# The matrices of a grouped state-space scan built with real and imaginary parts side by side in three vector operations, a sum of two scans handed to an adding DMA, and padded copies moved to ScalarE

## The chip, the cores and the metric

One core of a Trainium2 chip runs the whole program in one launch. Its engines run side by side, each through its own list in order: TensorE (PE, matrix products), VectorE (DVE), ScalarE (ACT), GpSimd (POOL) and SyncE (SP). Waits between them are semaphores. SP, ACT and POOL also issue DMAs, each from its own queue, and a DMA that waits holds everything behind it in that queue. The metric is device microseconds of one execution, lower is better. Everything is float32 in and out.

## The reference, cut to what matters

One block of a diffusion model: a mixer with two parallel head groups, then an MLP. The mixer's products `u @ w_in` give the inputs of an RG-LRU group (8 heads of 128 channels), its gates, and the inputs of an S5 group (64 channel groups of 16). Of the RG-LRU:

```python
def coeffs(xc):                       # xc: conv of 4 taps over time
    r = sigmoid(block_diag_linear(xc, wa, ba))
    i = sigmoid(block_diag_linear(xc, wi, bi))
    log_a = -8 * softplus(-lam) * r
    return exp(log_a), sqrt(-expm1(2 * log_a)) * (i * xc)
# linear scan forward and backward, each: 256 context steps, then 1024 latent steps
rg_lat = (hl_f + hl_b) * gelu(gate_lat)          # the sum of the two directions
```

Of the S5 group, per channel group g, with 64 complex states in two directions:

```python
lam_bar = exp(lam * dt)
b_bar = ((lam_bar - 1) / lam)[..., None] * (b_re + 1j * b_im)
bu = einsum("blgh,gph->blgp", u, b_bar)          # into the states
h = scan of h[t] = lam_bar * h[t - 1] + bu[t]
y = einsum("blgp,ghp->blgh", h, c_re + 1j * c_im).real
```

Then GELU, a gated linear unit, one output product `w_out`, a layer norm, and the MLP with a second norm.

## The kernel before, in words

Channels lie on the 128 partitions, time along the free dimension. float32 products are made of three passes: every operand is split into a high part and a rest (`wh`, `wl`, `x0h`, `x0l`; ScalarE casts the high part, L98, VectorE subtracts it, L47), and TensorE multiplies high by high, high by rest and rest by high. L47 is the line of the helper `tt`, through which nearly all two-operand VectorE work goes, so it is told apart by tile names. `x0h`, `x0l` are the latent tokens (512 columns a product), `x1h`, `x1l` the context (256).

S5 is not scanned step by step over time but in chunks of 8 tokens. For each of eight blocks m of 8 channel groups the kernel builds three things from the powers `pw` of `lam_bar`, the input matrix `bb` (b_bar) and the output matrix `cc`:
- X (`make_x`, `make_xt`, L487 to L514): `bb` times eight powers, complex, for four groups at a time: six operations of 128 x 512 on VectorE (`X0`, `X1`, temporary `Xt`), then eight transposes on TensorE (`ps_tr`, L510), ScalarE copies (`xt`, L511) and a store to memory. It is later the matrix that carries a chunk into the states.
- Y (`s5_taps`, L516 on): `cc` times eight powers, again four groups at a time, six operations (`Y`, temporary `yt`), with `cn`, the negated imaginary part; stored by SP as `yd` and later read as `yf`, the matrix from states to outputs.
- the taps inside a chunk: Y times a zero-padded copy `bz` of `bb` (8 small VectorE copies for each block, L561; products `ps_kt`, L566; ScalarE copy `kt`, L569).

These are interleaved with the RG-LRU heads in one stage (74 to 420 us). The program text calls its steps in the order of the string `X0 R0 T0 G2 S0 R1 X1 S1 T1 R2 X2 ... T3 X4 R4 ...` (L576), where R is a head (`rg_head`, L409), G the projection of a head's input (`proj_rgx`), S the projection of a block's S5 input (`proj_s5`); T is `s5_taps`, X is `make_xt`. From this text, a scheduler sets at build time each engine's list. Tiles of one tag with `bufs=1` share one buffer, so the next writer waits for the last reader.

A head R runs a chain. ScalarE and VectorE make the conv (`xc`: one activation, three multiply-adds, L56), ScalarE rounds it (`xch`, L421), VectorE forms the rest (`xcl`), TensorE makes 36 gate products (`ps_g`, L435), ScalarE takes sigmoids (`rr`, `ii`, L437), then, with two loads of its function table, Exp (`aa`, L442), Tanh (L443) and Sqrt (`rr`, L446); VectorE multiplies (`rr`, `ii`) and runs three scans (L455 to L458), and adds the two directions (`ii`, L47). The sum goes to memory as `hs` on SP's queue (L462; head 7's on POOL's). The next head's conv stands on VectorE among the scans of this one. The eight heads begin 41 to 46 us apart.

After the last head, `s5_in` (L592) loads X and the inputs, makes the products `ps_si` (L601) and copies them into `H` (the states of blocks 0 to 3 by ScalarE and VectorE, those of 4 to 7 by ScalarE alone). `scan` (L608) is some 128 dependent steps of three small VectorE operations for each half, preceded by a tree over the context (`sC`). Beside it TensorE makes the gates (`proj_gate`, `ge`; it reads `hs`) and the output products, then the S5 outputs `ps_so` (L751 to L753), which need `H`, and all that follows (norm, MLP), which the change does not touch.

Of the kernel before, what the change touches and what calls it, by code (L numbers as in the profile page):

```python
# [41 lines left out]
def build(nc, tc, a, out):  # L42
# [1421 lines left out]
```

## Time and profile before

| | |
|---|---|
| time, median of 3 runs | 1595.54 us (1594.12 to 1600.06) |
| the profiled execution | 1594.69 us, of it a span of 1592.9 us |
| TensorE busy | 1476.7 us (93%) |
| VectorE busy | 1256.8 us (79%) |
| ScalarE busy | 843.0 us (53%) |
| GpSimd busy | 71.0 us (4%) |
| mean granted TensorE clock | 0.974 of full |

Busy time is the time in which an engine ran at least one instruction; matmuls overlap in TensorE's pipeline, so a mean duration of 395 ns does not mean one each 395 ns. An average over the program hides its stages: the stage of the heads has TensorE and VectorE equally busy (326.90 us of 346 each, by chance the same figure), the scans that follow bind VectorE, and from about 680 us on TensorE hardly ever rests. A row of a wait names the engine and line that waited, and what came last.

### The profile page before, as it was taken

The numbers are of one execution on the slowest core, as the hardware profiler recorded it, in microseconds if no ns is written. First come the engines' busy times: TensorE is split into PE (matmuls) and PEld (weight loads), VectorE is DVE, ScalarE is ACT, GpSimd is POOL, SyncE is SP. The second block draws the span as 40 slices with busy tenths as digits, with TensorE's granted clock in tenths as the row PEclk, the third lists the DMA queues.
The fourth block names the chain that finished last, engine by engine and source line by source line (L and its number), as shares of the span: only waits on it lengthen the run. The fifth ranks groups of instructions, "written<-read, shape, count | busy, mean of one in ns | idle before, by whom it ended". The sixth has DMA issues, their size and how long they took to land. (4 is left out here: it accounts for less than half of the span.)

```text
span 1592.9 us, 20440 instructions
## 1 busy us (share of the span) xinstructions
PE 1476.7 (93%) x7148; PEld 1202.4 (75%) x7148; DVE 1256.8 (79%) x2555; ACT 843.0 (53%) x1178; POOL 71.0 (4%) x141
## 2 busy tenths in 40 slices
PE   7899998999978999699999799989899899999997
PEld 2687777778756878598878677867788788888886
DVE  7899999998866989635978789778787566667877
ACT  4675656666795331954233576444555554344425
POOL 0000000000000000000000011111111000000000
PEclk9999999999999999799999999999999999999999
DMA  7623323323664752983768576777764786776703
GB/s 255 233 94 119 115 99 120 105 106 119 231 215 137 209 183 91 264 201 119 228 207 265 173 242 232 279 248 268 245 219 167 268 287 215 263 251 210 240 7 106
DMA packets 131382, 304.16 MB, mean 191 GB/s; under 512 B 16208, under 2 KB 47440, under 8 KB 129872
## 3 DMA queue, kind: packets, MB, share of 16 engines
q1 hardware_dynamic: 104048, 237.45, 46.9%
q0 software_dynamic: 13184, 47.72, 8.4%
q10 hardware_dynamic: 14048, 17.70, 3.1%
q8 instruction: 56, 0.92, 0.2%
q14 instruction: 46, 0.38, 0.1%
HBM read 219.52 MB, written 83.30 MB: 190 GB/s over the span
## 5 line engine op out<-in xcount | busy, mean ns | idle before, releaser
L98 ACT CAST wh<-wr 128x1024 fp32r<-128x1024 f32 x113 | 118.4, 1051 | 230.0 <-PE ps_m L1276 73.8
L47 DVE TENSOR_TENSOR wl<-wr,wh 128x1024 fp32r<-128x1024 f32 (+1 forms) x161 | 170.5, 1060 | 83.7 <-ACT wh L98 77.2
L1066 PE MATMUL ps_m<-xt,wh 128*128 128x512 f32 x512 | 160.7, 395 | 0.0
L1276 PE MATMUL ps_m<-bh,wh 128*128 128x512 f32 x392 | 153.7, 392 | 3.8 <-ACT bh L1238 3.7
L1276 PE MATMUL ps_m<-bl,wh 128*128 128x512 f32 x392 | 153.4, 391 | 0.5 <-DVE bl L47 0.5
L1276 PE MATMUL ps_m<-bh,wl 128*128 128x512 f32 x392 | 153.3, 391 | 0.0
L380 PE MATMUL ps_mm<-x0h,wh 128*128 128x512 f32 x352 | 140.3, 399 | 1.0 <-ACT wh L98 1.0
L380 PE MATMUL ps_mm<-x0h,wl 128*128 128x512 f32 x352 | 140.0, 399 | 0.9 <-DVE wl L47 0.9
L380 PE MATMUL ps_mm<-x0l,wh 128*128 128x512 f32 x352 | 140.0, 398 | 0.0
L1066 PEld LDWEIGHTS ps_m<-xt,wh 128*128 128x128 f32 x512 | 97.5, 191 | 21.2 <-issue 0.3
L1066 PE MATMUL ps_m<-xt,wl 128*128 128x512 f32 x256 | 101.9, 398 | 10.5 <-DVE wl L47 10.5
L1276 PEld LDWEIGHTS ps_m<-bh,wh 128*128 128x128 f32 x392 | 73.8, 188 | 20.6 <-ACT bh L1238 4.1
L1276 PEld LDWEIGHTS ps_m<-bl,wh 128*128 128x128 f32 x392 | 74.0, 189 | 16.6 <-DVE bl L47 1.0
L1276 PEld LDWEIGHTS ps_m<-bh,wl 128*128 128x128 f32 x392 | 74.0, 189 | 15.5
L675 PE MATMUL ps_wo<-ms,wh 128*128 128x512 f32 x256 | 81.7, 400 | 2.7 <-ACT ms L799 2.7
L1066 PE MATMUL ps_m<-x,wh 128*128 128x512 f32 x256 | 81.8, 400 | 1.0 <-ACT wh L1149 1.0
L380 PEld LDWEIGHTS ps_mm<-x0h,wl 128*128 128x128 f32 x352 | 67.2, 191 | 14.3 <-DVE wl L47 1.4
L380 PEld LDWEIGHTS ps_mm<-x0h,wh 128*128 128x128 f32 x352 | 67.1, 191 | 13.5 <-ACT wh L98 1.4
L380 PEld LDWEIGHTS ps_mm<-x0l,wh 128*128 128x128 f32 x352 | 67.1, 191 | 12.5
L47 DVE TENSOR_TENSOR sT<-al,H 128x128 f32<-128x128 f32 x254 | 66.9, 286 | 1.3
L1066 PEld LDWEIGHTS ps_m<-xt,wl 128*128 128x128 f32 x256 | 49.0, 191 | 23.6 <-DVE wl L47 13.4
L47 DVE TENSOR_TENSOR bl<-br,bh 128x1024 fp32r<-128x1024 f32 x49 | 59.5, 1218 | 2.2 <-ACT bh L1238 2.2
(352 smaller groups left out, 3696.2 us busy)
## 6 DMA issues: line engine op xcount, KB each, us to landing
wr<-in_w SPq DMA_DIRECT2D x79, 512.0 KB, 5.2
br<-hq SPq DMA_DIRECT2D x49, 512.0 KB, 5.0
mo<-in_ada_t SPq DMA_DIRECT2D x32, 512.0 KB, 4.1
hq<-hs POOLq DMA_DIRECT2D x14, 1024.0 KB, 8.2
wr<-in_w_in SPq DMA_DIRECT2D x24, 512.0 KB, 4.3
wr<-in_w_out SPq DMA_DIRECT2D x24, 512.0 KB, 4.5
xt<-xt ACTq DMA_DIRECT2D x16, 512.0 KB, 2.7
yd<-Y SPq DMA_DIRECT2D x16, 512.0 KB, 2.6
```

The costliest lines, as they stand in the source:

```text
L47: (eng or V).tensor_tensor(out=o, in0=x, in1=y, op=op)
L98: S.copy(hi, raw)
L380: PE.matmul(ps, w[:, ks], x, start=(k == 0 and c == 0), stop=(k == KT - 1 and c == 2))
L675: PE.matmul(ps, u[:, ks], v[:, js], start=(c == 0), stop=(c == 3 * KT - 1))
L1066: PE.matmul(ps, u[:, ks], v, start=(first and c == 0), stop=(last and c == 11))
L1276: PE.matmul(pss[m], w[:, 512 * k + P * m:512 * k + P * m + P], x[:, 512 * k:512 * k + 512], start=(q == 0 and k == 0 and c == 0), stop=(q ...
```

## The change

What it does, part by part:

- The powers `pw`, the input matrix `bb` and the output matrix `cc` are laid out so that for each group the real and imaginary 16 columns lie side by side (32 columns), and `cc` carries a third block (the negated real part), so that rows 0 and 1 and rows 1 and 2 are the two operands. A complex product of four groups is then two multiplications and one addition of 128 x 1024 in place of six operations of 128 x 512, in `make_x` and in `s5_taps`.
- The negated parts and the padded copies are now ScalarE's: `bn` (an activation and a copy) for X; `bq` (a packed copy of `bb`), two activations on `cc` and four copies of `bz` per block, in place of VectorE's `cn` and its eight copies.
- X's temporaries now have the tags `Y` and `XY`, which Y uses too, one buffer each. (X's tiles print as `XY` and `XXY`: the letter X and the tag. Y's second one prints as `XY` too.)
- The sum of the two directions: the add on VectorE goes; POOL's queue stores the forward scan, and then issues a second DMA that adds the backward scan to it in memory.
- The powers of the scan (`a8`) are written to memory early, by SP, and read back by SP into a buffer that exists only from the scan on, ahead of the first loads of `s5_in`. The buffers of `xt` in `s5_in` go from 3 to 2.
- `yf` is read by the output products with 16 of 32 columns.

```diff
+    a8t = pp.tile([P, 5, 3, 64], F32, name="a8t")
...
+    a8d = dr.tile([P, 5, 3, 64], F32, name="a8d")
+    ld(a8d, a8t)
...
-        tt(it[0][:, NC:NT], it[0][:, NC:NT], it[1][:, NC:NT], ADD)
         d = dr.tile([P, NL], F32, name=f"hs{h}")
-        (nc.sync if h < 7 else G).dma_start(out=d, in_=it[0][:, NC:NT])
+        G.dma_start(out=d, in_=it[0][:, NC:NT])
+        G.dma_start(out=d, in_=it[1][:, NC:NT], accum_op=ADD)
...
-    def make_x(g0, n):
-
-        pr = [pw[:, i, 8:0:-1, g0:g0 + n].rearrange("p j g -> p g j").unsqueeze(3).to_broadcast([P, n, T8, 16]) for i in range(2)]
-        b = [bb[:, i, g0:g0 + n, :].unsqueeze(2).to_broadcast([P, n, T8, 16]) for i in range(2)]
-        xs = [ev.tile([P, n, T8, 16], F32, tag=f"X{i}", name=f"X{i}", bufs=1) for i in range(2)]
-        t = ev.tile([P, n, T8, 16], F32, tag="Xt", name="Xt", bufs=1)
-        tt(xs[0], pr[0], b[0], MUL)
+    def make_x(g0, n, bn):
+
+        pr = [pw[:, i, g0:g0 + n, 8:0:-1].unsqueeze(3).to_broadcast([P, n, T8, 32]) for i in range(2)]
+        b = [v.rearrange("p g r c -> p g (r c)").unsqueeze(2).to_broadcast([P, n, T8, 32]) for v in (bb[:, g0:g0 + n], bn)]
+        u, t = (ev.tile([P, n, T8, 32], F32, tag=g, name="X" + g, bufs=1) for g in ("Y", "XY"))
+        tt(u, pr[0], b[0], MUL)
         tt(t, pr[1], b[1], MUL)
-        tt(xs[0], xs[0], t, SUB)
-        tt(xs[1], pr[0], b[1], MUL)
-        t = ev.tile([P, n, T8, 16], F32, tag="Xt", name="Xt", bufs=1)
-        tt(t, pr[1], b[0], MUL)
-        tt(xs[1], xs[1], t, ADD)
-        return xs
+        x = ev.tile([P, 2, n * T8, 16], F32, tag="X", name="X", bufs=1)
+        u, t = (v.rearrange("p g t (r c) -> p (g t) r c", r=2) for v in (u, t))
+        tt(x.rearrange("p r k c -> p k r c"), u, t, ADD)
+        return x
...
+        bn = ev.tile([P, 8, 2, 16], F32, tag="bn", name="bn", bufs=1)
+        S.activation(bn[:, :, 0], bb[:, 8 * m:8 * m + 8, 1], AF.Copy, scale=-1.0)
+        S.copy(bn[:, :, 1], bb[:, 8 * m:8 * m + 8, 0])
         for q in range(2):
-            xs = make_x(m * 8 + q * 4, 4)
+            x = make_x(m * 8 + q * 4, 4, bn[:, 4 * q:4 * q + 4])
...
-        cc = ev.tile([P, 2, 8, 16], F32, tag="cc", name="cc", bufs=1)
-        ld(cc, a["s5c"][m])
-        cn = ev.tile([P, 8, 16], F32, tag="cn", name="cn", bufs=1)
-        ts(cn, cc[:, 1], -1.0, MUL)
+        bq = ev.tile([P, 2, P], F32, tag="bq", name="bq", bufs=1)
+        S.copy(bq.rearrange("p i (g c) -> p g i c", g=8), bb[:, g0:g0 + 8])
+
+        cc = ev.tile([P, 8, 3, 16], F32, tag="cc", name="cc", bufs=1)
+        ld(cc[:, :, 0:2], a["s5c"][m])
+        S.activation(cc[:, :, 1], cc[:, :, 1], AF.Copy, scale=-1.0)
+        S.activation(cc[:, :, 2], cc[:, :, 0], AF.Copy, scale=-1.0)
...
-            ys = ev.tile([P, 2, 4, T8, 16], F32, tag="Y", name="Y", bufs=1)
-            yt = ev.tile([P, 4, T8, 16], F32, tag="Yt", name="yt", bufs=1)
-            tt(ys[:, 0], cb(cc[:, 0]), pb(pw[:, 0]), MUL)
-            tt(yt, cb(cn), pb(pw[:, 1]), MUL)
-            tt(ys[:, 0], ys[:, 0], yt, ADD)
-            yt = ev.tile([P, 4, T8, 16], F32, tag="Yt", name="yt", bufs=1)
-            tt(yt, cb(cc[:, 0]), pb(pw[:, 1]), MUL)
-            tt(ys[:, 1], cb(cn), pb(pw[:, 0]), MUL)
-            tt(ys[:, 1], ys[:, 1], yt, SUB)
-            yf = ys.rearrange("p i g t c -> p i g (t c)")
-            ld(yscr[m][:, s], yf)
-            for i in range(2):
-                zv = bz[:, i].rearrange("p (g x) -> p g x", g=4)
-                for d in range(2):
-                    hs = slice(64 * d, 64 * d + 64)
-                    V.tensor_copy(zv[hs, :, 64 * d:64 * d + 16], bb[hs, i, g1:g1 + 4, :])
+            pr = [pw[:, i, g1:g1 + 4, 0:T8].unsqueeze(3).to_broadcast([P, 4, T8, 32]) for i in range(2)]
+            cs_ = [cc[:, gs_, i:i + 2].rearrange("p g r c -> p g (r c)").unsqueeze(2).to_broadcast([P, 4, T8, 32]) for i in range(2)]
+            ys, yt = (ev.tile([P, 4, T8, 32], F32, tag=g, name=g, bufs=1) for g in ("Y", "XY"))
+            tt(ys, cs_[0], pr[0], MUL)
+            tt(yt, cs_[1], pr[1], MUL)
+            tt(ys, ys, yt, ADD)
+            ld(yscr[m][:, s], ys)
+            zv = bz.rearrange("p i (g x) -> p i g x", g=4)
+            for d in range(2):
+                hs = slice(64 * d, 64 * d + 64)
+                S.copy(zv[hs, :, :, 64 * d:64 * d + 16], bb[hs, g1:g1 + 4].rearrange("p g r c -> p r g c"))
...
+    a8 = sc.tile([P, 5, 3, 64], F32, name="a8")
+    ld(a8, a8d)
...
-            xt = inp.tile([P, 4, 2, P], F32, tag="xt", name="xt", bufs=3)
+            xt = inp.tile([P, 4, 2, P], F32, tag="xt", name="xt", bufs=2)
```

The scheduler then sets other lists. First VectorE between head 3 and head 4 (head 3's scans on `ii_1879`, `ii_1880`, head 4's conv `xc_2240`), before:

```order
L56 SCALAR_TENSOR_TENSOR rr_1877<-aa_1881,rr_1877 128x1280
L56 SCALAR_TENSOR_TENSOR rr_1878<-aa_1882,rr_1878 128x1280
L47 TENSOR_TENSOR ii_1879<-ii_1879,rr_1877 128x1280
L47 TENSOR_TENSOR ii_1880<-ii_1880,rr_1878 128x1280
L455 SCALAR_TENSOR_TENSOR ii_1879<-aa_1881,ii_1879 128x1280
L457 SCALAR_TENSOR_TENSOR ii_1880<-aa_1882,ii_1880 128x256
L56 SCALAR_TENSOR_TENSOR xc_2240<-rx_1978,cols_70,xc_2240 128x1283
L458 SCALAR_TENSOR_TENSOR ii_1880<-aa_1882,ii_1880 128x1024
L56 SCALAR_TENSOR_TENSOR xc_2240<-rx_1978,cols_70,xc_2240 128x1283
L47 TENSOR_TENSOR ii_1879<-ii_1879,ii_1880 128x1024
L56 SCALAR_TENSOR_TENSOR xc_2240<-rx_1978,cols_70,xc_2240 128x1283
```

After, the same place (head 3's scans on `ii_1836`, `ii_1837`, head 4's conv `xc_2177`; the tiles `XY`, `XXY` and `X` are block 4's X):

```order
L47 TENSOR_TENSOR ii_1837<-ii_1837,rr_1835 128x1280
L457 SCALAR_TENSOR_TENSOR ii_1836<-aa_1838,ii_1836 128x1280
L459 SCALAR_TENSOR_TENSOR ii_1837<-aa_1839,ii_1837 128x256
L47 TENSOR_TENSOR XY_2129<-pw_152,bb_153 128x1024
L460 SCALAR_TENSOR_TENSOR ii_1837<-aa_1839,ii_1837 128x1024
L47 TENSOR_TENSOR X_2133<-XY_2129,XXY_2130 128x32x2x16
L56 SCALAR_TENSOR_TENSOR xc_2177<-rx_1935,cols_70,xc_2177 128x1283
L47 TENSOR_TENSOR XY_2150<-pw_152,bb_153 128x1024
L47 TENSOR_TENSOR XXY_2151<-pw_152,bn_2126 128x1024
L56 SCALAR_TENSOR_TENSOR xc_2177<-rx_1935,cols_70,xc_2177 128x1283
L47 TENSOR_TENSOR X_2154<-XY_2150,XXY_2151 128x32x2x16
L56 SCALAR_TENSOR_TENSOR xc_2177<-rx_1935,cols_70,xc_2177 128x1283
```

Five operations of X, 128 x 1024 each, now stand between the scans and the last `xc`; the add `ii_1879` is gone; the first weight rest `wl_2656` of the next S5 projection stands behind `xcl`.

Second TensorE just ahead of head 4's gate products, before:

```order
L380 MATMUL ps_mm_2553<-x0h7_714,wh_2497 128x512
L380 MATMUL ps_mm_2553<-x0l7_715,wh_2497 128x512
L380 MATMUL ps_mm_2553<-x0h7_714,wl_2498 128x512
L380 MATMUL ps_mm_2737<-x1h0_392,wh_2733 128x256
L380 MATMUL ps_mm_2737<-x1l0_393,wh_2733 128x256
L380 MATMUL ps_mm_2763<-x0h0_386,wh_2733 128x512
L380 MATMUL ps_mm_2763<-x0l0_387,wh_2733 128x512
L380 MATMUL ps_mm_2789<-x0h0_386,wh_2733 128x512
L380 MATMUL ps_mm_2789<-x0l0_387,wh_2733 128x512
L435 MATMUL ps_g_2255<-xch_2245,gwh_2251 128x256
L435 MATMUL ps_g_2260<-xch_2245,gwh_2251 128x512
```

And after:

```order
L382 MATMUL ps_mm_2480<-x0h7_716,wl_2425 128x512
L561 MATMUL ps_kt_2113<-Y_2105,bz_767 128x128 x8
L382 MATMUL ps_mm_2659<-x1h0_394,wh_2655 128x256
L382 MATMUL ps_mm_2659<-x1l0_395,wh_2655 128x256
L382 MATMUL ps_mm_2685<-x0h0_388,wh_2655 128x512
L382 MATMUL ps_mm_2685<-x0l0_389,wh_2655 128x512
L382 MATMUL ps_mm_2711<-x0h0_388,wh_2655 128x512
L513 MATMUL ps_tr_2136<-ident_71,X_2133 128x128 x4
L513 MATMUL ps_tr_2142<-ident_71,X_2133 128x128 x4
L382 MATMUL ps_mm_2711<-x0l0_389,wh_2655 128x512
L513 MATMUL ps_tr_2157<-ident_71,X_2154 128x128 x4
L513 MATMUL ps_tr_2163<-ident_71,X_2154 128x128 x4
```

Between the last `ps_g` of head 3 and the first of head 4 there were 68 products of 512 columns, 26 of 256 and 32 of 128; now there are 43, 2 and 34. At heads 1, 2, 3 and 5 the columns between the two grow by 1 to 3%, at head 6 by 17%, and at head 7 they shrink by 15%. The products that need `wl_2656` stand behind the gates of head 4.

## Rows read from the trace of the kernel before

**Rows 1.** Which engine is busy how long, by stretch of the program.

```profile
core 0: us, PE busy (x) PEld busy (x) DVE busy (x) ACT busy (x) POOL busy (x), PEclk, DMA share, GB/s
74.00:420.00 346.00, 326.90 (x1770) 271.44 (x1769) 326.90 (x439) 228.45 (x301) 1.02 (x18) 0.98 0.34 117
490.00:650.00 160.00, 155.34 (x677) 126.40 (x676) 151.17 (x742) 56.74 (x65) 4.30 (x5) 1.00 0.58 163
680.00:800.00 120.00, 119.90 (x704) 103.40 (x703) 72.17 (x97) 50.88 (x64) 0.00 (x0) 1.00 0.66 189
```

**Rows 2.** TensorE's waits between 74 and 420 us, line, releaser, total, times, longest.

```profile
PE ps_g L435 <- ACT xch L421: 13.8, 6, 3.0
PE ps_tr L510 <- DVE X L47: 2.2, 1, 2.2
PE ps_mm L380 <- ACT wh L98: 1.6, 1, 1.6
```

**Rows 3.** TensorE's timeline around the first and last gate products of heads.

```profile
232.32 0.39 PE L435 MATMUL ps_g<-xch,gwl 128*128 128x512 f32 x1
261.79 0.58 PE L435 MATMUL ps_g<-xch,gwh 128*128 128x256 f32 x1 [2.41 <-ACT xch L421]
315.38 0.39 PE L435 MATMUL ps_g<-xch,gwl 128*128 128x512 f32 x1
344.31 0.39 PE L435 MATMUL ps_g<-xch,gwh 128*128 128x256 f32 x1 [2.28 <-ACT xch L421]
```

**Rows 4.** ScalarE's timeline between two heads.

```profile
324.67 2.43 ACT L446 ACTIVATE rr<-rr 128x1280 f32<-128x1280 f32 x2
342.99 1.26 ACT L421 CAST xch<-xc 128x1283 fp32r<-128x1283 f32 x1 [2.62 <-DVE xc L56]
```

**Rows 5.** VectorE's timeline between the same two heads.

```profile
322.33 0.69 DVE L47 TENSOR_TENSOR Y<-cn,pw 128x512 f32<-128x512 f32 x1
322.94 0.69 DVE L47 TENSOR_TENSOR Y<-Y,yt 128x512 f32<-128x512 f32 x1
326.19 2.89 DVE L56 SCALAR_TENSOR_TENSOR rr<-aa,rr 128x1280 f32<-128x1280 f32 x2
340.28 1.22 DVE L47 TENSOR_TENSOR ii<-ii 128x1024 f32<-128x1024 f32 x1
341.41 1.54 DVE L56 SCALAR_TENSOR_TENSOR xc<-rx,cols,xc 128x1283 f32<-128x1283 f32 x1
```

**Rows 6.** VectorE's groups between 74 and 420 us, one shape each.

```profile
L47 DVE TENSOR_TENSOR Y<-Y,yt 128x512 f32<-128x512 f32 x32 | 22.0, 686 | 0.4
L47 DVE TENSOR_TENSOR wl<-wr,wh 128x1024 fp32r<-128x1024 f32 x16 | 19.4, 1217 | 0.0
L561 DVE COPY bz<-bb 64x64 f32<-64x64 f32 x64 | 11.9, 186 | 1.7 <-PE ps_kt L566 1.2
```

**Rows 7.** One of ScalarE's groups between 74 and 420 us.

```profile
L569 ACT COPY kt<-ps_kt 128x128 f32<-128x128 f32 x16 | 4.2, 262 | 3.8 <-DMA kp<-kt 3.6 <-ACT us L480 0.2
```

**Rows 8.** TensorE's granted clock in stretches of 6 us behind four waits.

```profile
129.00:135.00 6.00, 6.00 (x17) 4.83 (x18) 6.00 (x10) 3.08 (x4) 0.00 (x0) 0.50 0.00 0
217.40:223.40 6.00, 6.00 (x24) 4.94 (x25) 5.96 (x11) 2.50 (x4) 0.00 (x0) 0.74 0.01 3
261.80:267.80 6.00, 5.69 (x15) 3.89 (x16) 5.96 (x11) 4.38 (x6) 0.00 (x0) 0.50 0.22 87
344.40:350.40 6.00, 6.00 (x33) 4.94 (x34) 6.00 (x10) 3.75 (x6) 0.00 (x0) 1.00 0.01 3
```

**Rows 9.** VectorE's and ScalarE's timeline where the S5 scans start.

```profile
491.27 0.70 DVE L47 TENSOR_TENSOR sC<-a,H 128x512 f32<-128x512 f32 x1 [22.82 <-ACT H L605]
491.08 0.63 ACT L606 COPY H<-ps_si 64x256 f32<-64x256 f32 x1
```

**Rows 10.** DMA issues of the whole program, KB each, us to landing.

```profile
hq<-hs POOLq DMA_DIRECT2D x14, 1024.0 KB, 8.2
hs<-ii SPq DMA_DIRECT2D x7, 512.0 KB, 2.6
```

More of the change, by code (lines that the diff above doesn't have):

```diff
@@ L122, in build @@
     sp4 = con.tile([P, 16], F32, name="sp4")
-    a8 = con.tile([P, 5, 3, 64], F32, name="a8")
     c5 = con.tile([P, row(40)], F32, name="c5")
@@ L175, in build @@
     mods1(0, 4)
-    pw = prm.tile([P, 2, 9, 64], F32, name="pw")
-    bb = prm.tile([P, 2, 64, 16], F32, name="bb")
+    pw = prm.tile([P, 2, 64, 9], F32, name="pw")
+    bb = prm.tile([P, 64, 2, 16], F32, name="bb")
     qre, qim = (prm.tile([P, 64], F32, name=n) for n in ("qre", "qim"))
@@ L262, in build @@
         tt(oi, oi, pt[:, :n], ADD)
-    S.copy(pw[0:64], pl[0:64])
-    S.copy(pw[64:128], pl[64:128, :, ::-1, :])
+    S.copy(pw[0:64].rearrange("p i g j -> p i j g"), pl[0:64])
+    S.copy(pw[64:128].rearrange("p i g j -> p i j g"), pl[64:128, :, ::-1, :])
+    a8t = pp.tile([P, 5, 3, 64], F32, name="a8t")
     pr, pi = pl[:, 0, 8, :], pl[:, 1, 8, :]
@@ L356, in bc @@
         return q.unsqueeze(2).to_broadcast([P, 64, 16])
-    tt(bb[:, 0], sb[:, 0], bc(qre), MUL)
+    tt(bb[:, :, 0], sb[:, 0], bc(qre), MUL)
     tt(big, sb[:, 1], bc(qim), MUL)
-    tt(bb[:, 0], bb[:, 0], big, SUB)
-    tt(bb[:, 1], sb[:, 1], bc(qre), MUL)
+    tt(bb[:, :, 0], bb[:, :, 0], big, SUB)
+    tt(bb[:, :, 1], sb[:, 1], bc(qre), MUL)
     tt(big, sb[:, 0], bc(qim), MUL)
-    tt(bb[:, 1], bb[:, 1], big, ADD)
+    tt(bb[:, :, 1], bb[:, :, 1], big, ADD)
     st.close()
@@ L524, in s5_taps @@
         kp = kpscr[m // 2][m % 2]
-        yscr[m] = dr.tile([P, 2, 2, 4, P], F32, name=f"yd{m}")
+        yscr[m] = dr.tile([P, 2, 4, T8, 32], F32, name=f"yd{m}")
         pk = psx.tile([P, 8, 16], F32, tag="rg", name="ps_k0", bufs=2)
-        PE.matmul(pk, bb[:, 0, g0:g0 + 8, :].rearrange("p g c -> p (g c)"), cc[:, 0].rearrange("p g c -> p (g c)"), start=True, stop=False)
-        PE.matmul(pk, bb[:, 1, g0:g0 + 8, :].rearrange("p g c -> p (g c)"), cn.rearrange("p g c -> p (g c)"), start=False, stop=True)
+        for i in range(2):
+            PE.matmul(pk, bq[:, i], cc[:, :, i], start=(i == 0), stop=(i == 1))
         km = ev.tile([P, 8, 16], F32, tag="kt", name="km", bufs=1)
@@ L565, in s5_taps @@
                 for i in range(2):
-                    PE.matmul(pk, bz[:, i, g * P:(g + 1) * P], yf[:, i, g, :], start=(c == 0), stop=(c == 7))
+                    PE.matmul(pk, bz[:, i, g * P:(g + 1) * P], ys[:, g, :, 16 * i:16 * i + 16], start=(c == 0), stop=(c == 7))
                     c += 1
@@ L742, in s5_out @@
         ld(u2, uscr[m].rearrange("t (c g) n -> (t c) g n", g=8)[:, :, CC:NCH])
-        yf = sop[1].tile([P, 2, 2, 4, P], F32, tag="yf", name="yf", bufs=3)
+        yf = sop[1].tile([P, 2, 4, T8, 32], F32, tag="yf", name="yf", bufs=3)
         ld(yf, yscr[m])
@@ L751, in s5_out @@
                 PE.matmul(ps[:, g, :], u2[:, gl, :], mt[:, gl, :], start=True, stop=False)
-                PE.matmul(ps[:, g, :], h2[:, gl, 0, :], yf[:, s, 0, g, :], start=False, stop=False)
-                PE.matmul(ps[:, g, :], h2[:, gl, 1, :], yf[:, s, 1, g, :], start=False, stop=True)
+                PE.matmul(ps[:, g, :], h2[:, gl, 0, :], yf[:, s, g, :, 0:16], start=False, stop=False)
+                PE.matmul(ps[:, g, :], h2[:, gl, 1, :], yf[:, s, g, :, 16:32], start=False, stop=True)
             S.activation(gs[:, :, 4 * s:4 * s + 4].rearrange("n t g c -> n g t c"),
```

14 lines of the change are left out of this document (5 added, 9 removed).

## The prediction, made before the changed kernel had run

> **What bounds the kernel now.** I read the busy times by stretch first. From 680 us on TensorE is busy 119.90 of 120 us, and the edit leaves that part alone; from 490 to 650 VectorE (151.17 of 160) and TensorE share the load, since the scans are a chain of small VectorE operations [rows 1]. The edit lies in the stretch from 74 to 420 us, where TensorE and VectorE are both busy 326.90 of 346 us. Neither share says which of them is late, so I read TensorE's waits there next: 13.8 us in six waits of the first gate product of a head for `xch`, 2.2 for one X, 1.6 for one cast, 17.6 us in all [rows 2]. The timeline then shows what the longest of them is made of. From the end of the last gate product of head 3 (232.32 + 0.39) to the first of head 4 (261.79) pass 29.1 us; the same way between heads 5 and 6 (315.77 to 344.31) takes 28.5 [rows 3], and in all seven transitions it is 28.3 to 29.3. So a period is a chain of fixed length: ScalarE's functions until the square roots (324.67), VectorE's `rr` at 326.19, the scans mixed with the next conv, the last `xc` at 341.41, and at 342.99 ScalarE's `xch` [rows 4, 5]. TensorE fills that time with 45 to 53 thousand columns of other products, which takes it 25 to 28 us, and waits for what remains. VectorE is full beside this, but its `rr` starts only 0.3 us behind the end of the first square root (half of 2.43 past 324.67): less work on VectorE ahead of `rr` has almost nothing to pull forward.
>
> **The operations.** A 128 x 512 operation lasts 686 ns and a 128 x 1024 one 1217 [rows 6]. In the timeline the next one starts 0.61 us after the last (322.33, 322.94), not 0.69 [rows 5], so back to back six small ones cost 3.66 us and three large ones, with the same 0.08 overlap, 3.4: 0.25 saved, 32 times, 8 us. [...]
>
> Beside it VectorE loses 64 `bz` copies (11.9 us, [rows 6]), eight `cn` (below 2 us) and the adds of the two directions (1.22 each, [rows 5], eight times, 9.8 us). Some 30 of its 327 us go. ScalarE gains per block ten small operations; the nearest row is the copy of 128 x 128 at 262 ns [rows 7], so 2.6 us a block, 21 us on top of 228.45 of 346 [rows 1]. Most of them lie where ScalarE waits. A few, with a weight cast, now stand between the last sigmoids of a head; against that the cast of the gate weights has left that place. Bounds -3 and +6 us over the stage; I take +1.
>
> **The order.** The relief would be worth something if the list kept the chain as it was. Between heads 3 and 4 it does not. X shares the buffers of Y there, so block 4's X is built late, and five operations of it stand between the scans and the last `xc`; the add of 1.22 has left. At 1.14 each (1.217 less the overlap) the chain grows by 5 x 1.14 - 1.14 = 4.6 us, from 29.1 to 33.7. At the same place TensorE has less to do: before, 68 x 512 + 26 x 256 + 32 x 128 = 45.6 thousand columns, which took 29.1 less the waits of 2.41 [rows 3] and 1.6 [rows 2], 25.1 us, or 0.55 us a thousand. After, 43 x 512 + 2 x 256 + 34 x 128 = 26.9 thousand, 14.8 us. TensorE can do no more, since the rest of the projection needs `wl_2656`, which VectorE makes behind the chain. It stands still for 33.7 - 14.8 = 18.9 us, where it stood 4.0.
>
> At the other transitions I count the columns of the new list in the same way (50.7, 50.4 and 50.4 thousand ahead of heads 1 to 3, 49.7, 56.6 and 45.3 ahead of heads 5 to 7) at 0.54. The chain stays 28.4 to 28.9 (the add has left it, another small operation has mostly come in), and is 3.4 longer ahead of head 6, where three operations of Y stand in it. The waits are then 1.5, 1.2, 1.2, 1.6, 1.8 and 3.9 us. With 18.9 that makes 30.1 against 17.6: **+12.5 us**. The 0.25 us that VectorE saves per group does not enter: it ends in front of `rr`, or behind the chain.
>
> [...]
>
> **What is left.** The last add of a head, 1.22 us ahead of the copies of `s5_in`, goes: **-1.1**. The first operation of the second scan waits 22.82 us, until ScalarE's last copy into `H` (491.08) is done [rows 9]. The new list puts one gate activation and two weight casts more (some 2.7 us) ahead of that copy on ScalarE, and three weight subtractions, one gate product and two scan steps (some 5 us of VectorE) into the wait: **-2.3**, bounds -5 and +2.7. From there a shift passes through to the end, since scan, output product and norm follow each other. Early on, SP's store of `a8d` stands ahead of weight and input loads until VectorE has made it: 0 to 4 us, **+1**. The read back, ahead of the first load of `s5_in`, has TensorE's tail of head 7 as cover; if that is short, one transfer, at most the 8.2 us of the largest on POOL's queue [rows 10], is in the open; I take nothing.
>
> The two `hs` DMAs leave SP's queue for POOL's. The forward tile is free for the next head's sigmoids some 21 us past `rr`, the backward one some 27, and their DMAs start 8.4 and 12.5 us past `rr`; a plain `hs` landed in 2.6 us, and a store twice as long on POOL's queue in 8.2 [rows 10]. So it is hidden with 15 us for the adding one, of which no row shows the length. SP's queue no longer waits for the sums, so loads behind them can come earlier; the one wait of TensorE that this can help is the 1.6 us for a cast, already in the sum. Bounds 0 and, at twice 8.2, 1.4 us late a head, 10 us.
>
> **Sum.** 12.5 + 1 - 1.5 - 1.1 - 2.3 + 1 = +9.6, rounded to 9 as the columns' rate is good to some 3%. The profiled execution took 1594.69 us (span 1592.9 and 1.79 around it), 0.85 below the median of the three runs, 1595.54; on the median that is **1604.5 us**. Its own range, by these bounds, is 1594 to 1616.
>
> **Rivals.**
> 1. *VectorE's relief shortens every chain (faster).* For it: VectorE is busy to within a fraction of a microsecond of `rr`, and busy 326.90 of 346. Against it: the chain is 28.3 to 29.3 long whatever VectorE did in the period. [...] It decides from the point where `rr` starts over 1 us earlier, counted from the last gate product.
> 2. *Nothing shows.* The hole ahead of head 4 is filled because TensorE comes to head 3's gates late and has a backlog there, and the rest cancels: 1595. For it: the product counts of a period as a whole are the same. Against it: the hole is counted from the last gate product, which no backlog can pass in an in-order list.
> 3. *The adding DMA holds the sigmoids (still slower).* [...] No row shows an accumulating DMA. From over 15 us between issue and landing the `ii` sigmoids of the next head wait; at twice 8.2 us that is 10 us more than my sum, 1614, at three times 1660.
>
> **Chances.** Forecast 0.53, relief 0.22, nothing 0.15, DMA 0.10. What a measurement of this kernel can tell from no change is about 0.5%, 8 us, so the limits are 1587.6 and 1603.5. The forecast lies just past the upper one: of its 0.53 I give 0.29 to slower and 0.24 to the same. Relief gives 0.20 to faster and 0.02 to the same, nothing 0.12 to the same, 0.02 faster and 0.01 slower, the DMA 0.10 slower: 0.22 faster, 0.38 the same, 0.40 slower. The range 1582 to 1615 holds the forecast, the second rival and the nearer half of the others.
>
> **What would show it.** TensorE's wait ahead of head 4's first gate product: 15 us or more, released by `xch`, and half clock behind it; elsewhere waits of 1 to 4 us. From the last gate product to `rr` still 10.4 us (315.77 to 326.19). VectorE's busy time from 74 to the end of the stage near 300, with its idle time grown by as much. The first `ps_si` some 12 us later than before. No `ii` sigmoid waiting for a POOL DMA. I am wrong if the chain from the last gate product to the next `xch` is 3 us shorter at several heads, if the hole ahead of head 4 is below 8 us, or if the shift at `s5_in` does not reach the end.

## The result, and the profile after

The changed kernel takes 1620.45 us (median of 4 runs, 1616.09 to 1625.86), the kernel before in the same comparison 1594.83 (4 runs, 1593.04 to 1600.06): a ratio of 1.0157, 95% interval 1.0117 to 1.0197. It is slower by 25.6 us, where the forecast was 9 and its range ended at 1615. The profiled execution took 1616.09 us, the fastest of the four, with a span of 1614.2; that is 21.3 more than the span of before, and the profile is read against this figure.

First the busy times by stretch, with the columns of [rows 1]. The stretch from 74 to 420 us no longer ends at the same point of the program, so the first two rows, before and after, run from the start to VectorE's first copy into `H`, by which TensorE has done 1996 products in both. The third is of after, and answers to the last of [rows 1], shifted by the 20 us that the program runs late.

```profile
0.00:422.08 422.08, 386.37 (x1996) 304.42 (x1996) 386.03 (x661) 270.22 (x357) 2.56 (x29) 0.97 0.40 139
0.00:441.32 441.32, 387.69 (x1996) 311.26 (x1996) 361.58 (x486) 289.22 (x429) 13.28 (x44) 0.94 0.45 144
700.00:820.00 120.00, 119.90 (x712) 103.83 (x711) 72.57 (x98) 51.08 (x62) 0.00 (x0) 1.00 0.67 188
```

VectorE did lose 24.5 us (386.03 to 361.58; the prediction had some 30), and the stretch is 19.2 longer all the same. From 700 us on TensorE is as busy as it was. TensorE's waits between 74 and 420 us, as in [rows 2]:

```profile
PE ps_g L437 <- ACT xch L423: 11.9, 7, 2.4
PE ps_tr L513 <- DVE X L47: 6.2, 3, 4.0
PE ps_mm L382 <- ACT wh L98: 4.8, 1, 4.8
PE ps_kt L561 <- DVE Y L47: 2.3, 1, 2.3
PE ps_mm L382 <- ACT us L482: 2.0, 1, 2.0
PE ps_kt L561 <- ACT bz L556: 1.5, 1, 1.5
```

With three below 1 us they come to 30.2; the forecast had 30.1. (Before, with its three below 0.6 us, which the prediction's 17.6 leaves out, they come to 18.6.) So the largest term of the sum came out as forecast, and the time did not. VectorE's own waits, between 74 and 440 us, say what became of its relief:

```profile
DVE ii L47 <- ACT ii L439: 25.3, 18, 4.0
DVE rr L56 <- ACT rr L448: 23.5, 7, 4.4
```

Before it waited 7.6 and 2.9 us in these two places. It is idle until ScalarE's sigmoids and square roots are done, and no chain starts earlier for it. TensorE's timeline at heads 3 to 6, answering to [rows 3], with the waits between heads 3 and 4:

```profile
237.75 0.39 PE L437 MATMUL ps_g<-xch,gwl 128*128 128x512 f32 x1
250.73 2.05 PE L561 MATMUL ps_kt<-Y,bz 128*128 128x128 f32 x16 [1.46 <-ACT bz L556]
257.59 0.58 PE L382 MATMUL ps_mm<-x1h,wh 128*128 128x256 f32 x1 [4.81 <-ACT wh L98]
261.59 1.94 PE L513 MATMUL ps_tr<-ident,X 128*128 128x128 f32 x8 [1.92 <-DVE X L47]
267.93 1.94 PE L513 MATMUL ps_tr<-ident,X 128*128 128x128 f32 x8 [3.97 <-DVE X L47]
270.85 1.01 PE L437 MATMUL ps_g<-xch,gwh 128*128 128x256 f32 x2 [0.98 <-ACT xch L423]
326.69 0.39 PE L437 MATMUL ps_g<-xch,gwl 128*128 128x512 f32 x1
362.00 0.63 PE L437 MATMUL ps_g<-xch,gwh 128*128 128x256 f32 x2 [1.50 <-ACT xch L423]
```

The chain ahead of head 4 is 270.85 - 238.14 = 32.7 us (forecast 33.7). The hole is there, in five pieces of 13.1 us together rather than one of 18.9. Ahead of head 6 the chain is 362.00 - 327.08 = 34.9, where I had about 32 (28.4 to 28.9, and 3.4).

Where the time went shows when the stage is cut at the heads. The first gate product of a head starts its gate phase, which lasts until its 36th; from there to the next head's first is the chain. The end of head 7's gates is the start of head 0, plus eight gate phases, plus seven chains. That holds for any kernel: the cut says where time lies, and not yet why. These rows of before give the ends of the sum, VectorE's first copy into `H`, the start of the first scan, and the first S5 output (`ps_so`) that waits for its activation (`gs`), called the output below:

```profile
85.90 0.39 PE L435 MATMUL ps_g<-xch,gwh 128*128 128x256 f32 x1
398.83 0.39 PE L435 MATMUL ps_g<-xch,gwl 128*128 128x512 f32 x1
422.08 0.27 DVE L605 COPY H<-ps_si 64x64 f32<-64x64 f32 x1
445.19 0.75 DVE L47 TENSOR_TENSOR sC<-a,H 128x512 f32<-128x512 f32 x1
673.86 0.58 PE L751 MATMUL ps_so<-mt,u 128*128 128x128 f32 x1 [13.01 <-ACT gs L754]
```

And of after, with the second scan's start as in [rows 9]:

```profile
92.25 0.59 PE L437 MATMUL ps_g<-xch,gwh 128*128 128x256 f32 x2
419.33 0.39 PE L437 MATMUL ps_g<-xch,gwl 128*128 128x512 f32 x1
441.32 0.27 DVE L602 COPY H<-ps_si 64x64 f32<-64x64 f32 x1
468.96 0.75 DVE L47 TENSOR_TENSOR sC<-a,H 128x512 f32<-128x512 f32 x1
518.50 0.70 DVE L47 TENSOR_TENSOR sC<-a,H 128x512 f32<-128x512 f32 x1 [4.05 <-ACT H L602]
695.82 0.80 PE L748 MATMUL ps_so<-mt,u 128*128 128x128 f32 x2 [10.39 <-ACT gs L751]
```

Cut so, in us, for all kernels run (their edits follow below; `H` copy is VectorE's first, and the column after the chains is TensorE's idle time within gate phases and chains together):

| | start of head 0 | gate phases | chains | of both, TensorE idle | end of head 7's gates | to the first `H` copy | to the output | ratio |
|---|---|---|---|---|---|---|---|---|
| before | 85.9 | 111.1 | 202.2 | 18.6 | 399.2 | 22.9 | 251.8 | 1 |
| after | 92.3 | 120.4 | 207.0 | 28.9 | 419.7 | 21.6 | 254.5 | 1.0157 |
| e1 | 86.0 | 112.0 | 200.6 | 19.2 | 398.6 | 22.5 | 252.8 | 1.0007 |
| e2 | 91.8 | 122.7 | 203.5 | 21.4 | 418.1 | 21.6 | 257.7 | 1.0140 |
| e3 | 91.2 | 122.2 | 207.0 | 28.9 | 420.4 | 21.6 | 253.8 | 1.0155 |
| e4 | 91.5 | 121.0 | 199.3 | 25.7 | 411.8 | 21.6 | 254.5 | 1.0074 |
| e5 | 90.8 | 121.0 | 206.9 | 28.7 | 418.7 | 21.6 | 255.1 | 1.0133 |
| e6 | 90.2 | 114.1 | 208.5 | 19.0 | 412.9 | 21.6 | 253.7 | 1.0105 |
| e7 | 90.8 | 109.0 | 205.6 | 18.1 | 405.4 | 22.0 | 255.3 | 1.0067 |
| e8 | 88.6 | 113.7 | 206.1 | 20.0 | 408.5 | 21.6 | 256.6 | 1.0061 |
| e9 | 88.5 | 108.6 | 206.3 | 21.9 | 403.4 | 38.2 | 256.2 | 1.0148 |
| e10 | 86.2 | 108.3 | 201.1 | 22.3 | 395.6 | 31.5 | 257.9 | 1.0054 |

After against before: 6.35 (start) + 9.3 (gate phases) + 4.85 (chains) - 1.27 (to the first `H` copy) + 2.73 (to the output) = 21.96 us, against the 21.3 by which the span grew. The part behind that output, which the edit leaves alone, takes 917 to 926 us in the profiles of all these kernels, without a pattern.

The gate phases grew since TensorE's list has other products in them. Head 2's is the clearest; before and after, by stretch:

```profile
174.53:188.05 13.52, 13.52 (x64) 10.82 (x64) 13.40 (x22) 10.05 (x17) 0.00 (x0) 1.00 0.35 118
```

```profile
176.89:196.04 19.15, 19.15 (x101) 16.68 (x102) 13.70 (x13) 11.93 (x21) 0.00 (x0) 0.91 0.49 172
```

Of the 64 and the 101 products 36 are gate products. TensorE rests in neither: it works 5.6 us longer before the head's sigmoids have all their inputs (up to 1.7 of them, 0.09 of 19.15, by the clock), and the chain behind has its full length (28.05) all the same. The opposite happens behind head 7, from its last gate product to the first `ps_si`, before and after:

```profile
399.22:419.17 19.95, 19.80 (x104) 16.36 (x103) 16.03 (x20) 13.69 (x15) 0.00 (x0) 1.00 0.63 209
```

```profile
419.72:434.20 14.48, 12.69 (x75) 10.81 (x74) 9.18 (x10) 11.49 (x13) 0.00 (x0) 1.00 0.55 192
```

Seven us of TensorE's work have left that place, and it saves nothing there, as VectorE's copies into `H` stand behind head 7's scans in any case (21.6 us).

### The profile page after: what moved, and what is told of

Its sections match the earlier page's. It is cut to its first block, busy times and chain, and to the rows that moved or that the text cites. A ratio compares the mean times of both kernels' runs of the same rounds, so it can differ in the third digit from the quotient of the medians.

```text
span 1614.2 us, 20390 instructions
## 1 busy us (share of the span) xinstructions
PE 1482.9 (92%) x7148; PEld 1213.8 (75%) x7148; DVE 1234.1 (76%) x2379; ACT 862.0 (53%) x1250; POOL 81.8 (5%) x156
## 5 line engine op out<-in xcount | busy, mean ns | idle before, releaser
L598 PE MATMUL ps_si<-ub,xt 128*128 128x160 f32 x256 | 50.1, 342 | 18.4 <-ACT H L603 9.9
```

The source lines that it names most:

```text
L598: last_in[m] = PE.matmul(ps[:, i, :], xt[:, g, i, :], ub[:, 4 * q + g, :], start=True, stop=True)
```

## The experiments

Theory A after this cut: the loss is start, gate phases and chains, set by the lists; a kernel's time follows their sum. Theory B, in the expectations: TensorE's waits alone count. Other rivals: the adding DMA, the small operations on ScalarE, the S5 input, the early store. The kernel before took 1594.83 to 1599.29 us (medians) in the four comparisons, so ratios are compared here, and not times; the changed kernel's is 1.0157 [1.0117, 1.0197].

**e1, the adding DMA alone.** The kernel before with:

```diff
-        tt(it[0][:, NC:NT], it[0][:, NC:NT], it[1][:, NC:NT], ADD)
-        (nc.sync if h < 7 else G).dma_start(out=d, in_=it[0][:, NC:NT])
+        G.dma_start(out=d, in_=it[0][:, NC:NT])
+        G.dma_start(out=d, in_=it[1][:, NC:NT], accum_op=ADD)
```

> The kernel before with one part of the change alone: the sum of the two directions by an adding DMA on POOL's queue, no add on VectorE. Theory (the adding DMA is hidden, and the change's loss comes from where the other operations were put): the add of 1.22 us leaves the chain of each head, a small operation of 0.6 us takes its place in the list, so each of seven chains is about 0.5 us shorter, and the last add is gone: 4 to 5 us faster than before, about 1590. Rival (the adding DMA holds the sigmoids of the next head, or disturbs other transfers): 1605 or more, with a wait of ScalarE's ii for a POOL DMA.

Measured: 1599.38 us against 1599.11, ratio 1.0007 [0.9984, 1.0029]. The two kinds of `hs` DMA together landed in 5.1 us (median), far from the 15 that would reach the sigmoids:

```profile
hs<-ii POOLq DMA_DIRECT2D x16, 512.0 KB, 5.1
```

No sigmoid waits for them. So the adding DMA does not carry the loss; with the lost add it is neutral to 0.3%. The 4 to 5 us that I expected did not come: the chains are 1.6 us shorter together, not 3.5, and the lost add gives 0.4 us behind head 7, where VectorE's first copy into `H` now waits 0.92 us for one of ScalarE's.

**e2, the small operations on VectorE.** The changed kernel, with `bn`, `bq`, the two on `cc` and `bz` made by VectorE:

```diff
-                S.copy(zv[hs, :, :, 64 * d:64 * d + 16], ...)
+                V.tensor_copy(zv[hs, :, :, 64 * d:64 * d + 16], ...)
```

> The changed kernel with all small operations (bn, bq, the negated cc, bz) on VectorE again, nothing else undone. Theory A (the loss is the chain of each head: where VectorE and ScalarE operations stand in it, and how many products stand among the gate products): the list now has no long chain between heads 5 and 6 (28 in place of 34.9 us), and 15.4 in place of 31.2 thousand columns among the gates of head 7 (some 7 us less), against 12 thousand more among the others (6 us more); about 8 us faster than the changed kernel, 1612. Theory B (TensorE's waits alone count): they fall from 30 to 14 us by the columns, so 16 us faster, 1604. Rival C (VectorE's relief was worth something): 20 us of work back on VectorE make it slower than the changed kernel, 1625 or more.

Measured: 1622.87 us, 1.0140 [1.0103, 1.0177]. The chain ahead of head 6 falls from 34.9 to 27.4 us, but the gate phases grow by 2.3, and the part behind the first `H` copy by 3.2. So neither theory's gain came: A had 8 us, B 16, and TensorE does stand still 7.5 us less within the heads (28.9 to 21.4) without a gain in time. The small operations on ScalarE can account for that chain alone, and what is gained there the new lists give back elsewhere. VectorE's work, put back, does not make the kernel slower than the changed one either.

**e3, three `xt` buffers in the S5 input.** The changed kernel with `bufs=3` for `xt` in `s5_in`.

> The changed kernel with three buffers for xt in s5_in again. The lists of the heads stay as in the changed kernel; among the products of s5_in there are again 24 gate products and no longer 48. Theory: the first half of s5_in takes 23 us in place of 27.6 (4.5 less), and what the gates did in the wait ahead of the second scan comes back behind it (2.5 more): 2 us faster than the changed kernel, 1618. Rival (the two buffers make the loads late, and both halves suffer): 6 to 9 us faster, 1612.

Measured: 1621.37 us, 1.0155 [1.0108, 1.0203]. The first scan starts 2.8 us earlier (466.13), the second waits 22.56 us as before, and the output comes at 695.72, against 695.82. The 2 us expected are not there, nor the rival's 6 to 9: the buffer does not carry the loss.

**e4, one step of the order.** The changed kernel with block 4's X called behind head 4:

```diff
-    for o in ('... X3 T3 X4 R4 T4 S3 ...').split():
+    for o in ('... X3 T3 R4 X4 T4 S3 ...').split():
```

> The changed kernel with block 4's X called after head 4 in the program text (R4 X4 in place of X4 R4). In the lists no operation of X stands between the scans of head 3 and head 4's conv any more, TensorE has 24.8 thousand columns there (before 26.9), and the gates of head 4 have 28.2 thousand columns among them (before 19.7). Theory A (chains and gate phases): chain ahead of head 4 28 in place of 32.7 us, gate phase of head 4 4 us longer, of head 7 2 us shorter, together 2 to 3 us faster than the changed kernel, 1617. Theory B (TensorE's waits by the columns, 23 in place of 30): 7 us faster, 1613.

Measured: 1610.79 us, 1.0074 [1.0052, 1.0096]. The chain ahead of head 4 is 27.4 us, that ahead of head 6 32.4. The end of head 7's gates comes 7.9 us earlier; 7.7 of that are the chains. TensorE still waits there, for the head itself:

```profile
265.08 1.01 PE L437 MATMUL ps_g<-xch,gwh 128*128 128x256 f32 x2 [5.43 <-ACT xch L423]
```

So the hole does not price the step: 11.7 of its 13.1 us are left, and the end comes earlier by about what the chains are shorter. The profiled gain, 7.95 us at the output, is past the 2 to 3 of theory A, which did not have the 2.5 us at head 6. It is near the 7 of theory B, but not by B's means: TensorE's idle time within the heads falls by 3.2 us (28.9 to 25.7).

**e5, the early store on POOL's queue.** The changed kernel with:

```diff
-    ld(a8d, a8t)
+    G.dma_start(out=a8d, in_=a8t)
```

> The changed kernel with the early store of a8d issued by POOL in place of SP. The lists of the heads stay as they are; on SP one load of the inputs stands again ahead of three weight loads. Theory: 2.5 of the 6 us by which head 0 starts late (bb's first product 68.4 in place of 65.9 us) come from that store, so 2.5 us faster than the changed kernel, 1618. Rival (the late start is VectorE's order alone, two X in front of head 0's xch): no difference, 1620.

Measured: 1618.97 us, 1.0133 [1.0115, 1.0151]. Head 0 starts 1.5 us earlier (expected 2.5); at the output 0.4 are left. The early store is a small part.

**e6, a buffer of its own for X's temporary.** The changed kernel; to make room `xt` is halved and `bn` and `bq` share a buffer:

```diff
-        u, t = (ev.tile([P, n, T8, 32], F32, tag=g, name="X" + g, bufs=1) for g in ("Y", "XY"))
+        u, t = (ev.tile([P, n, T8, 32], F32, tag=g, name="X" + g, bufs=1) for g in ("XA", "XY"))
-            xt = ev.tile([P, 4, 2, P], F32, tag="xt", name="xt", bufs=1)
+                xt = ev.tile([P, 2, 2, P], F32, tag="xt", name="xt", bufs=1)
-        bq = ev.tile([P, 2, P], F32, tag="bq", name="bq", bufs=1)
+        bq = ev.tile([P, 2, P], F32, tag="bn", name="bq", bufs=1)
```

> The changed kernel with a buffer of its own for the first temporary of X (tag XA in place of Y); the room is found by a half as large xt, stored in halves, and one buffer for bn and bq. In the new lists 214 thousand columns stand in the gate phases of the eight heads (231 in the changed kernel, 209 before), the chains ahead of heads 4 and 6 still hold five and six operations of X and Y. Theory (gate phases and chains make the stage long): 17 thousand columns at 0.49 us are 8 us, so 1612. Rival (TensorE's waits by the columns, 13 in place of 30): 17 us, 1603. Rival (the buffer has nothing to do with it): 1620.

Measured: 1612.64 us, 1.0105 [1.0077, 1.0132]. The end of head 7's gates comes 6.8 us earlier: gate phases -6.3, start -2.0, chains +1.5. Head 2's gate phase is 14.25 us with 75 products:

```profile
172.93:187.18 14.25, 14.25 (x75) 11.82 (x76) 14.22 (x14) 10.39 (x18) 0.00 (x0) 1.00 0.36 129
```

The two long chains stay (32.9 and 35.7). So here the gate phases make the gain, about the 8 us of the theory. TensorE is idle for 19.0 us within the heads, hardly more than before (18.6), and yet their end comes 13.7 us later than before: the waits do not say what the order costs. The interval of the ratio still overlaps that of the changed kernel; those of e4, e7 and e8 do not.

**e7, both.** e6 with e2's edit.

> The same buffer of its own for X, and the small operations (bn, bq, negated cc, bz) on VectorE. In the new lists 211 thousand columns stand in the gate phases (231 in the changed kernel), and no chain is longer than 30 us. Theory: 10 us from the gate phases, 5 from head 4's chain, 6 from head 6's, together 21 us faster than the changed kernel, 1600; the late start of head 0 (6 us) stays. Rival (small operations on VectorE or ScalarE, shared or not, make no difference): 1618.

Measured: 1606.11 us, 1.0067 [1.0042, 1.0092]. The end of head 7's gates comes 14.3 us earlier: gate phases -11.5, chains -1.4, start -1.4. Of the 21 us expected a third is missing: the two long chains give up 8.9 us, but the other five grow by 7.5, to between 28.2 and 30.8.

**e8, head 0 first.** e7 with e5's store on POOL's queue, and `R0 X0` in place of `X0 R0` in the order.

> As the kernel with X's own buffer and the small operations on VectorE, with two more edits for the start: a8d stored by POOL, and head 0 called before block 0's X in the program text. TensorE has 97.8 thousand columns ahead of head 0 (103.4 in the changed kernel, 96.3 before). Theory: head 0 starts at 86 us as before, 6 us earlier than in the changed kernel, so 27 us faster than that, 1594, level with the kernel before. Rival (the three wide operations in place of six, or the adding DMA, cost by themselves): 1602 or more, the stage of the heads longer than before in spite of a list like it.

Measured: 1605.52 us, 1.0061 [1.0043, 1.0079]; the same as e7. The start gains 2.2 us, the gate phases lose 4.8. Missed: one step moved at the start changed the lists far behind it. The time lies where the rival has it (1602 or more). In e7 to e9 the chains are 3.4 to 4.2 us longer than before, and no kernel here has the wide operations alone, so whether they cost something by themselves stays open.

**e9, an order searched for the sum.** e8 with three `xt` buffers, and the order chosen by the smallest start, gate phases and chains that a count in the lists gave:

```diff
-    for o in ('R0 X0 T0 G2 S0 R1 X1 S1 ... X4 R4 T4 ... G7 X7 S5 T6 R7 T7 S6 S7').split():
+    for o in ('R0 T0 X0 S0 R1 X1 G2 S1 ... X4 G5 R4 T4 ... G7 S5 T6 R7 S6 T7 X7 S7').split():
```

> The wide S5 matrices and the adding DMA with X's own buffer, the small operations on VectorE, a8d by POOL, three xt buffers, and another order of the steps in the program text (R0 T0 X0 S0 R1 X1 G2 ... S5 T6 R7 S6 T7 X7 S7). By the sum of start, gate phases and chains (0.54 us a thousand columns ahead of head 0, 0.49 in a gate phase, 28.3 us a chain and what VectorE's list adds) the stage is 355.5 us, before 360.6, changed kernel 379.8. Theory (that sum decides): 5 us less than before until the first copy into H, some 3 us of it lost in the S5 part as in the other kernels of this kind: 1593 to 1597. Rival (the wide operations cost by themselves, some 6 us beyond the list, as in the kernel with head 0 first): 1600 or more.

Measured: 1622.25 us, 1.0148 [1.0131, 1.0166]. Missed twice. The end of head 7's gates comes at 403.4, 4.2 us later than before, where the count had 5 earlier. And the first `H` copy comes 38.2 us behind it: X7 is last, and ScalarE's copies wait for the stores that have its one buffer:

```profile
425.68 0.59 ACT L515 COPY xt<-ps_tr 128x512 f32<-128x512 f32 x1 [7.13 <-DMA xt<-xt]
435.93 0.58 ACT L515 COPY xt<-ps_tr 128x512 f32<-128x512 f32 x1 [9.67 <-DMA xt<-xt]
```

**e10, the same for e1.** e1 with an order chosen in the same way, which leaves the last three projections for the end:

```diff
-    for o in ('X0 R0 T0 G2 S0 R1 X1 S1 T1 R2 X2 G3 S2 T2 R3 G4 X3 T3 X4 ... G7 X7 S5 T6 R7 T7 S6 S7').split():
+    for o in ('X0 R0 T0 G2 S0 R1 X1 T1 R2 X2 G3 S1 S2 T2 R3 X3 T3 G4 X4 ... G7 T6 X7 R7 T7 S5 S6 S7').split():
```

> The kernel before with the adding DMA alone and another order of the steps in the program text (R1 X1 T1 R2 X2 G3 S1 S2 ... T6 X7 R7 T7 S5 S6 S7). By the sum of start, gate phases and chains 352.3 us, before 360.6, with the adding DMA alone 357.5. Theory (that sum decides): 5 us faster than the adding DMA alone, so 4 to 6 us faster than before, 1592. Rival (the rest of the program takes back what the stage gains): level with before, 1597.

Measured: 1605.87 us, 1.0054 [1.0035, 1.0073]. The end of head 7's gates comes at 395.6, 3.6 us earlier than before, where the count had 8.3. And TensorE then has 160 products ahead of the first `ps_si`, where before it had 104:

```profile
395.57:425.60 30.03, 29.82 (x160) 25.50 (x159) 18.68 (x25) 16.16 (x19) 1.44 (x2) 1.00 0.64 197
```

So e9 and e10 show what the cut at the heads leaves out: behind head 7 the later of two ends counts, its scans (21.6 us, 22.9 with the add) or what TensorE and ScalarE have left. They also show the limit of theory A as a tool: the count in the lists missed the end of the heads by 9 and 5 us. In the changed kernel and its seven variants with a tail of 21.6 to 22.0 us, the end of head 7's gates, measured against before, lies within the interval of the ratio in seven of eight, and for e7 just below it (6.2 us are 1.0039, its interval starts at 1.0042). None of these kernels is faster than the one before, and the 10 us that e7 and e8 still lose are not taken apart.

## Why the prediction was wrong

The sign was right, and at head 4 the chain grew by about what was forecast (to 32.7 us, forecast 33.7); the size was 9 us for 25.6 (22 in the profile).

**The step that failed** is "With 18.9 that makes 30.1 against 17.6: +12.5 us", taken as the whole price of the order. The waits came to 30.2. But waits of TensorE are the whole price only if it does the same work up to the point where the stage is cut, or if what it does earlier shortens what follows. Its time up to the end of head 7's gates, before and after:

```profile
0.00:399.22 399.22, 364.23 (x1878) 285.97 (x1878) 367.13 (x636) 254.77 (x339) 2.56 (x29) 0.97 0.39 136
0.00:419.72 419.72, 372.67 (x1908) 298.36 (x1908) 345.33 (x468) 273.82 (x410) 12.72 (x43) 0.94 0.45 141
```

It stands still 12.1 us longer (34.99 to 47.05), as forecast, and it works 8.4 us longer, which the sum had at nothing. Thirty products more are done by then, and 29 fewer behind it (104 became 75). They are no gain there, since the tail is bound by the scans. Together that is 20.5 us, where the terms of the sum up to this point (12.5 + 1 + 1 - 1.5) make 13.0. The other large miss is the S5 part, 5.0 us, below; the tail's -1.1 was right. So 9.6 + 7.5 + 5.0 - 0.1 makes the 22.0 measured.

I counted columns between the gates, and neither those ahead of head 0 (103.4 thousand in place of 96.3) nor those within the gate phases. There the list has 231 thousand in place of 209 thousand, and the phases are 9.3 us longer with hardly a wait in them (0.6 us, before 0.3). The same prediction had found a chain of fixed length between the last gate product and the next head's `xch`; from that follows a sum over starts, gate phases and chains, and I did not make it. In e6 and e7 the gate phases are what shrinks, by 6.3 and 11.5 us, and the end comes 6.8 and 14.3 earlier; in e4 it is the chains.

That the waits agreed to 0.1 us is in part luck: the hole ahead of head 4 was 5.8 us smaller than forecast, and the waits of the other six chains 15.2 us and not 11.2.

**ScalarE, +1.** At one place it was 3 more. Ahead of head 6 `xc` is ready at 356.99, but ScalarE's list has other work in front of `xch`, and that waits for loads (and, at 357.59, for a product); some rows in between are left out:

```profile
351.78 0.31 ACT L526 ACTIVATE cc<-cc 128x128 f32<-128x128 f32 x1 [3.98 <-DMA cc<-in_s5c]
355.04 0.60 ACT L556 COPY bz<-bb 64x128 f32<-64x128 f32 x2 [0.99 <-issue]
359.74 1.05 ACT L98 CAST wh<-wr 128x1024 fp32r<-128x1024 f32 x1 [1.53 <-DMA wr<-in_w_in]
360.70 1.25 ACT L423 CAST xch<-xc 128x1283 fp32r<-128x1283 f32 x1
```

Elsewhere the moved operations cost nothing that shows, as e2 takes them off ScalarE again and gains nothing; I took a mean for something that counts at one place.

**The early store, +1.** Head 0 starts 6.35 us late. The bounds I gave were 0 to 4, for the store alone, and e5 gives 1.5 us back. The store stands in SP's queue ahead of later loads, which I had; SP issues nothing from 23.66 us until it, at 30.71:

```profile
30.71 0.33 SPq L59 DMA_DIRECT2D a8d<-a8t  x1
32.01 4.34 SPq L59 DMA_DIRECT2D aw<-in_ada_n  x3
36.40 0.42 SPq L59 DMA_DIRECT2D xr<-in_xT  x1
```

Before, that `xr` load, the third, was issued at 24.40. VectorE's timeline divides the loss: `bb`'s first product starts 2.5 us later (65.92, now 68.43), and head 0's last `xc` 6.4 us later (82.67, now 89.04). Between the two stood six operations of block 0's X of 128 x 512, one half; now both halves stand there, six of 128 x 1024, at 1.14 us each in place of 0.61 some 3.2 us more (an estimate from [rows 5, 6]). So block 0's X ahead of head 0, which the term did not have, is the larger part. Head 0 called first (e8) gives 2.2 us.

**The S5 input and the scans, -2.3.** From VectorE's first `H` copy to the output 2.7 us were lost, where the second scan's wait was to give 2.3 back. That wait did shrink (22.82 to 4.05), but since other work came into it: the second scan starts 49.5 us behind the first, before 46.1. And the first scan starts 27.6 us behind the `H` copy, before 23.1. From the second scan's start to the output 5.3 us come back. A third `xt` buffer (e3) takes 3.5 of the first 4.5 off, and the wait is 22.56 again, but from the second scan's start to the output it takes 183.8 us, before 182.6: 2.0 us are lost in all. The kernels with the wide operations lose 1.9 to 5.9 us in this part, but e10, which has none, loses 6.1. What does it stays open.

**The clock, -1.5.** No run shows this term, a loss of time to a lower clock behind TensorE's waits. What the runs show is the clock granted there: in the changed kernel the 6 us from the first gate product of heads 1 to 7 have 1.00, 0.72, 1.00, 0.50, 0.74, 1.00 and 1.00, behind waits for `xch` of 2.37, 2.32, 2.25, 0.98, 2.25, 1.50 and 0.19 us, so the length of the wait does not tell the clock. Behind head 4's it was 0.50, as forecast. Ahead of head 7 the waits were 2.2 us and not 3.9. The stretch around the hole, and those behind the waits of heads 4 and 7:

```profile
254.00:272.00 18.00, 7.39 (x24) 5.22 (x24) 18.00 (x14) 7.42 (x15) 1.59 (x5) 0.57 0.41 104
270.90:276.90 6.00, 5.42 (x17) 4.14 (x18) 5.97 (x6) 4.71 (x7) 0.00 (x0) 0.50 0.59 215
404.83:410.83 6.00, 6.00 (x29) 5.01 (x30) 6.00 (x6) 3.46 (x6) 0.00 (x0) 1.00 0.27 96
```

The first row goes with a hole of 13.1 us and not 18.9: the clock was low inside it too (0.57), and the products there took 32.7 - 13.1 = 19.6 us, not 14.8. The chain did not get longer by that. Head 4's gate phase took 13.1 us, before 12.6 at about the same clock (0.76, before 0.74, over the phase), so at this place the clock adds nothing to the loss. If time were lost in proportion to the missing clock, an estimate that no run tests, the stretches of 0.72, 0.50 and 0.74 would cost 6.2 us, and the first three of [rows 8] 7.6.

**Right:** the adding DMA is hidden (e1); the last add was worth 1.3 us behind head 7 (in e1 alone 0.4); VectorE's relief ahead of `rr` is worth nothing, as the time from the last gate product to `rr` is still 10.3 us (327.08 to 337.35):

```profile
337.35 2.89 DVE L56 SCALAR_TENSOR_TENSOR rr<-aa,rr 128x1280 f32<-128x1280 f32 x2
```

Ahead of heads 1, 2, 3, 5 and 7 the chain is 0.7 to 1.4 us shorter. In e1, where the add of 1.22 us alone has left it, it is 0.2 to 0.5 shorter at six heads and 0.3 longer at one; what else shortens it was not taken apart.

One VectorE operation of 128 x 1024 takes 1.22 us in the changed kernel (`XY`, at 262.82), where two of 128 x 512 took 2 x 0.69 before [rows 6]. No time came of it here.

Of the rivals, the first (faster) falls on these 10.3 us, the second (nothing shows) on the 25.6 us, the third on e1. e4 and e6 change the lists as a whole, so the price of one buffer or one step is not told apart from what the scheduler did with it. What is shown is that the order alone, with the same operations on the same engines, is worth half of the loss (e4), and a buffer of its own with the small operations on VectorE somewhat more than half (e7). The rest, with the S5 part, is open.

## What to carry to other kernels

Where a stage is a row of latency chains, cut it at the chains and sum start, phases and chains; the waits of a busy engine don't price it, since filler that moves ahead of a chain costs time without a wait showing (head 2's gate phase, 13.52 us before and 19.15 after, TensorE at work throughout), and if the tail is bound by something else nothing comes back there. The cut finds the time after a run; as a forecast from the lists it was off by 5 to 9 us here. Then look at the tail separately: the later of the last chain and the work left over ends it. Fewer operations on an engine that waits for its inputs are worth little unless they stood in the chain (VectorE had 24.5 us less to do here, in a stretch that grew by 19.2), and two helpers that come to share a buffer can change the order of a whole stage (with a buffer of its own, e6, head 7's gates end 6.8 us earlier).

## Not expected of the hardware

ScalarE is held by stores that it issues: while two `kp` stores are issued, 1.10 us together, it is idle for 0.98 us ahead of its next copy, ten times between 74 and 440 us, 9.1 us in all, where copies of 0.3 us were counted as cheap. The rows of the timeline, and that of the waits:

```profile
249.24 1.10 ACTq L65 DMA_DIRECT2D kp<-kt  x2
250.38 0.29 ACT L556 COPY bz<-bb 64x128 f32<-64x128 f32 x1 [0.98 <-issue]
```

```profile
ACT bz L556 <- issue: 9.1, 10, 1.0
```

The adding DMA takes POOL 0.2 to 0.3 us longer to issue than the plain one ahead of it, here at head 1 of e1, and no sigmoid waited for it:

```profile
163.90 0.56 POOL L461 DMA_DIRECT2D hs<-ii  x1 [36.30 <-ACT wh L98]
168.17 0.86 POOL L462 DMA_DIRECT2D hs<-ii  x1 [3.72 <-DVE ii L458]
```
